# A two-layer streaming encoder whose VectorE runs in written order

## The chip, the cores and the metric

One core of a Trainium2 chip. The metric is the device time of one execution in microseconds (us), median of several runs. Engines: PE (TensorE, matmuls), DVE (VectorE), ACT (ScalarE), POOL (GpSimd), SP (SyncE, which issues the DMAs).

## The reference

One inference step of a hybrid encoder, float32, DEPTH = 2 layers, D_MODEL = 1024, on 512 frames of a new stream and 8 streams of 16 frames that go on from a cache: 640 columns in all. A layer, cut to what matters:

```python
h = rmsnorm(x, g_pre_mix)
u = h @ w_in                                   # conv, q, kv, z, x/B/C, dt and 3 gates
a = u_glu[..., :D_CONV] * jax.nn.sigmoid(u_glu[..., D_CONV:])
c = jax.nn.silu(layernorm(causal_dwconv(a_pad, conv_w, conv_b), conv_ln_g, conv_ln_b))   # 31 taps
o = attention(rmsnorm(u_q, g_q) @ w_uq, ...)   # latent attention, softmax over chunks
y = ssd(...)                                   # Mamba-2 scan in chunks of 64, then a gated rmsnorm
merged = gates[..., 0, :] * o_conv + gates[..., 1, :] * o_attn + gates[..., 2, :] * o_ssm
x = x + rmsnorm(merged @ w_out, g_post_mix)
f = rmsnorm(x, g_pre_ffn) @ w_gate_up
f = (jax.nn.silu(f[..., :D_FF]) * f[..., D_FF:]) @ w_down
x = x + rmsnorm(f, g_post_ffn)
```

## The kernel before, in words

**Data and matmuls.** Activations lie transposed, as 8 blocks of 128 channels x 640 columns, and are worked on in two halves of 256 (half 0) and 384 columns (half 1). Every matmul of a weight is made of three: weights and activations are split into a high and a low part (`split`, L141: ACT copies the high part, L142, and DVE or POOL subtracts it from the source, L136), and `mm3` (L122) sums high x high, high x low and low x high. Tiles named wh, hh, fh are high parts, wl, hl, fl low parts (wbh, wbl: weights in a second pool).

**Units.** A `Unit` (L215) is 128 output columns of a weight: `load` fetches it in pieces of 128x512 (`raw`) and splits them, on POOL or DVE as its argument `eng` says; `run(half)` puts 24 matmuls into one of four PSUM buffers (`pg`) and calls the unit's `evac`, which reads it. The feed-forward units of the first six column blocks (`gu`, L1308) alternate POOL and DVE for the split of their weights.

**Interleaving.** Beside the units the kernel writes small programs as generators in lanes: attention (`attn`), state-space scan (`ssd`) and its norm (`yn`), convolution taps (`convp`, `conv`, `sc`), and the norms at the edges of a sub-layer (`bar`, `bar2`). After each unit, `pump` (L269) lets each lane advance by its rate, so the order in which the kernel writes its instructions is a mixture set by these rates:

```python
        u.run(half, k == "B")
        ...
        pump(0.5 * u.nk / 8)
```

**Who orders what.** The framework under the kernel takes the written instructions, adds the semaphores and, before the change, reorders the instructions of every engine by a scheduler of its own. Each engine then takes its list in order.

**Names in the prediction.**
- `task_conv` (L898): 23 of the 31 taps of the depthwise convolution, each two `scalar_tensor_tensor` on DVE (through `stt`, L139): `cv<-pp`, 128x512, and its twin `cv<-sp`, 128x128, for the samples. Nobody reads the result until the branch's layernorm. `task_sconv` (L973) does the same for the scan's 4 taps (`sa`).
- `rsqrt` (L178): 12 tiny DVE operations in a chain (`rv`, `ri`, then `ry` and `ra` three times over), with a 13th at L191 where it has a factor. It reads a column sum `cs` of PE (`colsum`, L172), and PE spreads its result over the partitions as `rb` (`bcast`, L194).
- `task_attn` (L617): softmax with `p` (L646 to L648), which PE transposes (`tp`, L657). `q_unit` (L567) makes `qf`, the normed q. `ecs` is a decay of the scan.
- `barrier` (L322): the last projection before a norm runs as all half 0, then all half 1. `sq_acc` (L400) squares each result on ACT (`sq`) and sums the squares on DVE (`acc`). `postnorm` (L410) takes the column sum of acc, rsqrt and rb, then per block a product on DVE and an addition of the residual `xl` (`mo` after the mixer, `dn` after the feed-forward), then squares and a tree of sums (`psq`, L376). `prenorm` (L384) takes their column sum and rsqrt, then per block `ht` (DVE, L394) and its split into `hh` and `hl`. `bar_mix` (L1298) chains both for the mixer's end, and `bar_ffn` (L1341) for the end of the feed-forward part.
- `fg`: the evacuation of a gate or up unit (`gu`).

Of the kernel before, what the change touches and what calls it, by code (L numbers as in the profile page):

```python
# [1574 lines left out]
@with_exitstack  # L1575
def hybrid_encoder_kernel(ctx: ExitStack, tc: tile.TileContext, I, O):
    emit(tc, ctx, I, O)


def build(nc, arrays):  # L1580
    I = {k: nc.dram_tensor("in_" + k, v.shape, mybir.dt.from_np(v.dtype), kind="ExternalInput").ap() for k, v in arrays.items()}
    O = {k: nc.dram_tensor("out_" + k, s, F32, kind="ExternalOutput").ap() for k, s in _OUTS.items()}
    with tile.TileContext(nc) as tc:
        hybrid_encoder_kernel(tc, I, O)


def _unlayout(r):
# [26 lines left out]
```

## Time and profile before

| what | value |
|---|---|
| median of 3 runs | 2809.32 us (2806.63 to 2812.78) |
| profiled execution | 2803.95 us |
| its span in the trace | 2802.2 us |
| mean granted clock of PE | 0.984 |
| instructions | 47677 |
| DVE busy | 1541.8 us, 3334 instructions |
| ACT busy | 1095.5 us |
| POOL busy | 1031.5 us |

Times in the trace are from the span's start. Layer 0's mixer reaches to about 975 us, its feed-forward part to about 1475, layer 1's mixer to about 2370, its feed-forward part to the end. [...]

### The profile page before, as it was taken

How to read it: one execution, taken by the hardware profiler on the slowest of the kernel's cores; microseconds unless marked ns; L12 is line 12 of the kernel's file. 1: busy time of each engine (PE TensorE's matmuls, PEld its weight loads, DVE VectorE, ACT ScalarE, POOL GpSimd, SP SyncE). 2: the span in 40 equal slices, each digit the busy share in tenths (PEclk: the TensorE clock that was granted, in tenths of full speed). 3: DMA queues.
4: the chain of work that ended last, by engine and by line, in shares of the span. 5: the costliest groups of instructions: out<-in, count | busy, mean ns of one | idle time of the engine just before them, and what ended most of it. 6: DMA issues, size and time to landing. Idle time of an engine off the chain costs nothing. (4 is left out here: it accounts for less than half of the span.)

```text
span 2802.2 us, 47677 instructions
## 1 busy us (share of the span) xinstructions
PE 2677.2 (96%) x17652; PEld 2571.6 (92%) x17652; DVE 1541.8 (55%) x3334; ACT 1095.5 (39%) x2436; POOL 1031.5 (37%) x992
## 2 busy tenths in 40 slices
PE   6989989999999899999979999999999999999998
PEld 6988888989999899999979888888989998999998
DVE  6464678485575732333573747676565656323334
ACT  4434543543334532222444344544443244322222
POOL 5563545544435400000565444545534353000004
PEclk9999999999999999999989999999999999999999
DMA  5353232534554422222444532334436444322224
GB/s 155 113 175 111 84 113 92 171 101 143 177 185 136 157 83 75 73 78 75 124 151 129 164 102 89 117 115 135 139 101 227 133 129 154 91 76 71 79 71 131
DMA packets 248538, 337.82 MB, mean 121 GB/s; under 512 B 52465, under 2 KB 139057, under 8 KB 248305
## 3 DMA queue, kind: packets, MB, share of 16 engines
q1 hardware_dynamic: 246720, 333.75, 38.3%
q8 instruction: 139, 2.28, 0.3%
q10 hardware_dynamic: 1584, 1.02, 0.1%
q14 instruction: 95, 0.77, 0.1%
HBM read 268.73 MB, written 65.94 MB: 119 GB/s over the span
## 5 line engine op out<-in xcount | busy, mean ns | idle before, releaser
L136 POOL TENSOR_TENSOR wl<-raw,wh 128x512 fp32r<-128x512 f32 (+2 forms) x470 | 634.4, 1356 | 1487.1 <-ACT wh L142 1440.9
L120 PE MATMUL pg<-hh,wh 128*128 128x256 f32 (+1 forms) x3296 | 1051.7, 319 | 6.3 <-ACT hh L142 4.7
L120 PE MATMUL pg<-hh,wl 128*128 128x256 f32 (+1 forms) x3296 | 1029.2, 313 | 8.3 <-DVE wl L136 7.9
L120 PE MATMUL pg<-hl,wh 128*128 128x256 f32 (+1 forms) x3296 | 1031.0, 313 | 3.0 <-DVE hl L136 1.7
L142 ACT CAST wh<-raw 128x512 fp32r<-128x512 f32 (+1 forms) x696 | 422.6, 610 | 862.6 <-PE pg L120 763.8
L120 PEld LDWEIGHTS pg<-hh,wh 128*128 128x128 f32 x3296 | 632.8, 192 | 13.0 <-ACT hh L142 5.2
L120 PEld LDWEIGHTS pg<-hh,wl 128*128 128x128 f32 x3296 | 633.0, 192 | 9.6 <-DVE wl L136 8.7
L120 PEld LDWEIGHTS pg<-hl,wh 128*128 128x128 f32 x3296 | 633.0, 192 | 8.4 <-DVE hl L136 3.4
L136 DVE TENSOR_TENSOR wl<-raw,wh 128x512 fp32r<-128x512 f32 (+1 forms) x226 | 154.6, 684 | 293.7 <-ACT wh L142 293.5
L120 PE MATMUL pg<-fh,wh 128*128 128x256 f32 (+1 forms) x648 | 200.6, 310 | 0.0
L120 PE MATMUL pg<-fl,wh 128*128 128x256 f32 (+1 forms) x648 | 200.2, 309 | 0.0
L120 PE MATMUL pg<-fh,wl 128*128 128x256 f32 (+1 forms) x648 | 200.1, 309 | 0.0
L139 DVE SCALAR_TENSOR_TENSOR cv<-pp,pk,cv 128x512 f32<-128x512 f32 x184 | 152.4, 829 | 13.5 <-POOL cv L136 13.5
L120 PEld LDWEIGHTS pg<-fl,wh 128*128 128x128 f32 x648 | 122.0, 188 | 0.0
L120 PEld LDWEIGHTS pg<-fh,wl 128*128 128x128 f32 x648 | 121.9, 188 | 0.0
L120 PEld LDWEIGHTS pg<-fh,wh 128*128 128x128 f32 x648 | 121.9, 188 | 0.0
L136 POOL TENSOR_TENSOR cv<-cv,cvt 128x640 f32<-128x640 f32 x56 | 89.2, 1593 | 84.8 <-ACT cvt L893 74.7
L139 DVE SCALAR_TENSOR_TENSOR sa<-pd,pk,sa 128x664 f32<-128x664 f32 x96 | 100.9, 1052 | 15.3 <-ACT sa L982 14.3
L136 DVE TENSOR_TENSOR acc<-acc,sq 128x256 f32<-128x256 f32 (+1 forms) x96 | 65.1, 680 | 72.4 <-ACT sq L407 71.6
L136 DVE TENSOR_TENSOR fg<-fg,pg 128x256 f32<-128x256 f32 (+1 forms) x88 | 42.8, 486 | 98.3 <-PE pg L120 98.3
L139 DVE SCALAR_TENSOR_TENSOR cv<-sp,pk,cv 128x128 f32<-128x128 f32 x184 | 86.4, 469 | 0.0
L142 ACT CAST fh<-fg 128x256 fp32r<-128x256 f32 (+1 forms) x88 | 40.5, 460 | 107.4 <-DVE fg L136 104.2
(309 smaller groups left out, 4595.7 us busy)
## 6 DMA issues: line engine op xcount, KB each, us to landing
raw<-in_w_in SPq DMA_DIRECT2D x284, 256.0 KB, 2.9
raw<-in_w_gu SPq DMA_DIRECT2D x208, 256.0 KB, 2.7
raw<-in_w_down SPq DMA_DIRECT2D x72, 256.0 KB, 2.7
raw<-in_w_mix SPq DMA_DIRECT2D x64, 256.0 KB, 2.9
ma<-gd SPq DMA_DIRECT2D x48, 320.0 KB, 4.3
raw<-in_w_out SPq DMA_DIRECT2D x48, 256.0 KB, 2.8
gd<-gs SPq DMA_DIRECT2D x48, 192.0 KB, 2.4
hb<-in_state_ssm SPq DMA_DIRECT2D x64, 128.0 KB, 2.9
```

The source lines that it names most:

```text
L120: nc.tensor.matmul(ps, l, r, start=a, stop=b)
L136: eng.tensor_tensor(o, a, b, op=op)
L139: V.scalar_tensor_tensor(o, a, s, b, op0=op0, op1=op1)
L142: nc.scalar.copy(hi, src)
```

## The change

The kernel's body is written inside a context that tells the scheduler to leave DVE alone: DVE takes its instructions in the order in which the kernel writes them. The other engines are still ordered by the scheduler. No instruction of PE, DVE, ACT, POOL or of the DMAs is added or taken away.

```diff
--- before.py
+++ after.py
@@ -1581,7 +1581,8 @@
     I = {k: nc.dram_tensor("in_" + k, v.shape, mybir.dt.from_np(v.dtype), kind="ExternalInput").ap() for k, v in arrays.items()}
     O = {k: nc.dram_tensor("out_" + k, s, F32, kind="ExternalOutput").ap() for k, s in _OUTS.items()}
     with tile.TileContext(nc) as tc:
-        hybrid_encoder_kernel(tc, I, O)
+        with tc.manual_schedule(engines={mybir.EngineType.DVE}):
+            hybrid_encoder_kernel(tc, I, O)
 
 
 def _unlayout(r):
```

DVE's list has 3334 working instructions before and after, of which 1083 change their place relative to the rest (PE: 350 of 16520, by at most 41 places; ACT 289 of 2367; POOL 80; SP 144). Three places, with what was before first. In a row, the names are those of the section above, with the number of the tile and of its buffer's use.

**DVE in the middle of layer 0, two rsqrt chains (ry_1017 and ry_1021) that PE waits for.** Before:

```order
L136 TENSOR_TENSOR ra_1022_4776<-ra_1022_4776,rv_1019_4770 128x3
L139 SCALAR_TENSOR_TENSOR cv_879_4108<-pp_861_4023,pk_28_132,cv_879_4108 128x512
L136 TENSOR_TENSOR ra_1018_4759<-ra_1018_4759,rv_1015_4753 128x2
L139 SCALAR_TENSOR_TENSOR ry_1021_4774<-ra_1022_4776,ry_1021_4774 128x3
L139 SCALAR_TENSOR_TENSOR cv_879_4108<-sp_862_4024,pk_28_132,cv_879_4108 128x128
L139 SCALAR_TENSOR_TENSOR ry_1017_4757<-ra_1018_4759,ry_1017_4757 128x2
L139 SCALAR_TENSOR_TENSOR ra_1022_4776<-ry_1021_4774 128x3
L139 SCALAR_TENSOR_TENSOR cv_879_4108<-pp_861_4023,pk_28_132,cv_879_4108 128x512
L191 TENSOR_SCALAR ry_1017_4757<-ry_1017_4757 128x2
L136 TENSOR_TENSOR ra_1022_4776<-ra_1022_4776,rv_1019_4770 128x3
```

With the change:

```order
L136 TENSOR_TENSOR ra_1018_4761<-ra_1018_4761,rv_1015_4755 128x2
L139 SCALAR_TENSOR_TENSOR ry_1017_4759<-ra_1018_4761,ry_1017_4759 128x2
L139 SCALAR_TENSOR_TENSOR ra_1018_4761<-ry_1017_4759 128x2
L136 TENSOR_TENSOR ra_1018_4761<-ra_1018_4761,rv_1015_4755 128x2
L139 SCALAR_TENSOR_TENSOR ry_1017_4759<-ra_1018_4761,ry_1017_4759 128x2
L139 SCALAR_TENSOR_TENSOR ra_1018_4761<-ry_1017_4759 128x2
L136 TENSOR_TENSOR ra_1018_4761<-ra_1018_4761,rv_1015_4755 128x2
L139 SCALAR_TENSOR_TENSOR ry_1017_4759<-ra_1018_4761,ry_1017_4759 128x2
L191 TENSOR_SCALAR ry_1017_4759<-ry_1017_4759 128x2
L180 TENSOR_SCALAR rv_1019_4772<-cs_1014_4751 128x3
```

The taps (cv_879) that stood between the links are gone from here, and the second chain follows the first instead of being threaded into it.

**DVE at layer 0's mix barrier, the rsqrt of half 0's postnorm (rv_2141).** Before:

```order
L136 TENSOR_TENSOR acc_2064_9831<-acc_2064_9831,sq_2118_10082 128x256
L136 TENSOR_TENSOR acc_2064_9831<-acc_2064_9831,sq_2127_10124 128x256
L180 TENSOR_SCALAR rv_2141_10203<-cs_2130_10155 128x2
L182 TENSOR_SCALAR ri_2142_10205<-rv_2141_10203 128x2
L184 TENSOR_SCALAR ry_2143_10207<-ri_2142_10205 128x2
L139 SCALAR_TENSOR_TENSOR ra_2144_10209<-ry_2143_10207 128x2
L136 TENSOR_TENSOR ra_2144_10209<-ra_2144_10209,rv_2141_10203 128x2
```

With the change:

```order
L136 TENSOR_TENSOR acc_2064_9833<-acc_2064_9833,sq_2118_10084 128x256
L136 TENSOR_TENSOR acc_2064_9833<-acc_2064_9833,sq_2127_10126 128x256
L136 TENSOR_TENSOR acc_2129_10155<-acc_2129_10155,sq_2140_10202 128x384
L180 TENSOR_SCALAR rv_2141_10205<-cs_2130_10157 128x2
L182 TENSOR_SCALAR ri_2142_10207<-rv_2141_10205 128x2
L184 TENSOR_SCALAR ry_2143_10209<-ri_2142_10207 128x2
L139 SCALAR_TENSOR_TENSOR ra_2144_10211<-ry_2143_10209 128x2
```

The first partial sum of squares of half 1, acc_2129 (from sq_2140), has come ahead of the chain.

**DVE a little later in the same barrier, the low part wl_2265 of the first gate/up weights.** Before, in the middle of half 1's rsqrt chain (ry_2249):

```order
L136 TENSOR_TENSOR fg_2228_10599<-fg_2228_10599,pg_2244_10634 128x256
L139 SCALAR_TENSOR_TENSOR ry_2249_10668<-ra_2250_10670,ry_2249_10668 128x3
L136 TENSOR_TENSOR wl_2265_10740<-raw_2263_10737,wh_2264_10739 128x512
L136 TENSOR_TENSOR fl_2246_10660<-fg_2228_10599,fh_2245_10659 128x256
L139 SCALAR_TENSOR_TENSOR ra_2250_10670<-ry_2249_10668 128x3
```

With the change:

```order
L136 TENSOR_TENSOR psq_2258_10708<-psq_2258_10708,psq_2259_10709 128x384
L136 TENSOR_TENSOR psq_2252_10702<-psq_2252_10702,psq_2254_10704 128x384
L136 TENSOR_TENSOR psq_2256_10706<-psq_2256_10706,psq_2258_10708 128x384
L136 TENSOR_TENSOR psq_2252_10702<-psq_2252_10702,psq_2256_10706 128x384
L136 TENSOR_TENSOR wl_2265_10742<-raw_2263_10739,wh_2264_10741 128x512
L139 SCALAR_TENSOR_TENSOR fg_2268_10771<-ft_2267_10770,pg_2266_10745 128x256
L136 TENSOR_TENSOR wl_2274_10783<-raw_2272_10780,wh_2273_10782 128x512
```

It now stands behind the tree of sums psq_2252, the last of half 1's postnorm. **PE** with the change, around the column sum cs_2287 of that tree:

```order
L120 MATMUL pg_2284_10828<-hl_2167_10338,wh_2264_10741 128x256
L120 MATMUL pg_2294_10873<-hh_2158_10329,wh_2270_10776 128x256
L120 MATMUL pg_2294_10873<-hl_2159_10330,wh_2270_10776 128x256
L120 MATMUL cs_2287_10857<-c_ones_111,psq_2252_10702 128x1 x3
L120 MATMUL pg_2294_10873<-hh_2158_10329,wl_2271_10777 128x256
L120 MATMUL pg_2284_10828<-hh_2166_10337,wl_2265_10742 128x256
```

Before, cs_2287 stood 41 rows further down, in a later unit, behind all matmuls with wl_2265; now it stands ahead of them, in the middle of units pg_2284 and pg_2294.

## Rows read from the trace of the kernel before

**Rows 1.** The page, part 1: busy time, share of the span, instructions.

```profile
PE 2677.2 (96%) x17652; PEld 2571.6 (92%) x17652; DVE 1541.8 (55%) x3334; ACT 1095.5 (39%) x2436; POOL 1031.5 (37%) x992
```

**Rows 2.** Stretches by stage: length, busy us of PE, PEld, DVE, ACT, POOL, granted clock, DMA.

```profile
100.00:880.00 780.00, 750.31 (x4915) 702.78 (x4914) 495.21 (x1099) 333.25 (x783) 377.01 (x377) 0.99 0.42 131
880.00:975.00 95.00, 87.23 (x601) 85.36 (x601) 68.59 (x153) 47.81 (x105) 47.63 (x40) 0.98 0.50 160
975.00:1375.00 400.00, 400.00 (x2705) 400.00 (x2704) 140.28 (x248) 118.82 (x227) 31.18 (x27) 1.00 0.27 82
1375.00:1475.00 100.00, 84.13 (x541) 82.36 (x540) 71.19 (x163) 44.42 (x98) 60.64 (x51) 0.90 0.49 151
1475.00:2270.00 795.00, 768.50 (x5030) 719.04 (x5030) 484.99 (x1102) 340.20 (x797) 381.05 (x384) 0.99 0.42 132
2270.00:2370.00 100.00, 92.95 (x605) 91.11 (x604) 70.56 (x157) 47.38 (x102) 44.65 (x38) 0.95 0.49 156
```

**Rows 3.** PE's waits, 100 to 880 us: us in total, times, longest.

```profile
PE tp L657 <- DVE p L648: 8.1, 5, 4.2
...
PE rb L120 <- DVE ry L191: 3.6, 2, 2.3
...
PE pg L120 <- DVE qf L136: 2.7, 3, 2.0
PE rb L120 <- DVE ry L139: 1.8, 1, 1.8
```

**Rows 4.** The same, 1475 to 2270 us.

```profile
PE tp L657 <- DVE p L648: 4.4, 2, 3.6
PE rb L120 <- DVE ry L139: 4.3, 1, 4.3
PE opt L792 <- DVE ecs L139: 3.9, 1, 3.9
PE rb L120 <- DVE ry L191: 2.4, 2, 1.6
PE pg L120 <- DVE qf L136: 2.0, 2, 1.8
```

**Rows 5.** DVE's timeline in layer 0's middle: start, length, engine, line, operation.

```profile
439.22 0.15 DVE L139 SCALAR_TENSOR_TENSOR ra<-ry 128x3 f32<-128x3 f32 x1
439.29 0.74 DVE L139 SCALAR_TENSOR_TENSOR cv<-pp,pk,cv 128x512 f32<-128x512 f32 x1
...
440.03 0.15 DVE L136 TENSOR_TENSOR ra<-ra,rv 128x3 f32<-128x3 f32 x1
440.10 0.34 DVE L139 SCALAR_TENSOR_TENSOR cv<-sp,pk,cv 128x128 f32<-128x128 f32 x1
```

**Rows 6.** Three stretches of 10 us, columns as in rows 2.

```profile
440.00:450.00 10.00, 7.46 (x36) 7.16 (x37) 9.44 (x28) 0.85 (x2) 1.64 (x1) 0.83 0.31 116
940.00:950.00 10.00, 6.29 (x42) 6.08 (x40) 6.52 (x12) 5.15 (x12) 4.88 (x5) 0.83 0.66 217
1738.00:1748.00 10.00, 6.36 (x31) 6.29 (x31) 9.04 (x23) 4.47 (x10) 4.54 (x6) 0.66 0.52 145
```

**Rows 7.** DVE's timeline, layer 0's mix barrier, postnorm of half 0.

```profile
890.17 0.16 DVE L180 TENSOR_SCALAR rv<-cs 128x2 f32<-128x2 f32 x1 [2.33 <-PE cs L120]
...
893.11 1.14 DVE L136 TENSOR_TENSOR ra<-ra,rv 128x2 f32<-128x2 f32 x1
...
896.10 0.94 DVE L136 TENSOR_TENSOR acc<-acc,sq 128x384 f32<-128x384 f32 x1
```

**Rows 8.** The same, half 1, in order of time.

```profile
930.45 0.69 DVE L136 TENSOR_TENSOR wl<-raw,wh 128x512 fp32r<-128x512 f32 x1 [0.21 <-ACT wh L142]
...
947.26 0.55 DVE L136 TENSOR_TENSOR psq<-psq,psq 128x384 f32<-128x384 f32 x1
...
956.73 0.69 DVE L136 TENSOR_TENSOR wl<-raw,wh 128x512 fp32r<-128x512 f32 x1
...
964.97 0.60 DVE L139 SCALAR_TENSOR_TENSOR ht<-mo,pk,rb 128x384 f32<-128x384 f32 x1
```

**Rows 9.** PE's timeline in the same barrier: a matmul and the wait before it.

```profile
945.79 0.58 PE L120 MATMUL pg<-hh,wl 128*128 128x256 f32 x1 [3.71 <-DVE wl L136]
```

## The prediction

> **What bounds the kernel now.** I read the page's busy times first, then the stretches by stage, then who TensorE (PE) waited for in each stretch, then the timeline of VectorE (DVE) at those places. PE is busy for 2677.2 of 2802.2 us, DVE for 1541.8 [rows 1]. So PE is the bound, and DVE's order can only act through PE's idle time, 2802.2 − 2677.2 = 125 us, or through the clock that PE is granted. The stretches say where that idle time lies [rows 2]: none of it in 975 to 1375 us, the feed-forward matmuls, where PE is busy for 400.00 of 400.00 us; 7.8 us in 880 to 975 (the change from mixer to feed-forward, "mix barrier" below), 15.9 us in 1375 to 1475 (from feed-forward to the next layer) and 7.1 us in 2270 to 2370 (layer 1's mix barrier). About 30 us more lies in the middle of layer 0 and 27 us in that of layer 1, where attention, convolutions and the state-space branch run between the weight units.
>
> The profiled execution took 2803.95 us, 5.4 us under the median of the runs, 2809.32. The sum below is a difference made inside that one execution; I add it to the median.
>
> **What goes: taps ahead of short chains, in the middle of the layers.** In the middle stretches the waits of PE that a DVE instruction ended are mostly on the softmax result p (8.1 us in layer 0, 4.4 in layer 1), on the rsqrt chains (`ry`: 3.6 + 1.8, then 4.3 + 2.4), on qf (2.7, 2.0) and on ecs (3.9) [rows 3, 4], 33.2 us in all. The timeline shows why they were late [rows 5]: between two 0.15 us links of a rsqrt chain stands a convolution tap of 0.74 us with its 0.34 us twin for the samples, though no one waits for that tap for a long time. In the written order the chain stands unbroken and the taps come behind it (first piece of order above). I laid the recorded durations of DVE into the new order, every instruction starting when its operands of before were there and the one ahead was done, and read how much earlier the awaited instruction ends, up to the length of PE's gap. Softmax gives 0.6 + 1.3 + 3.2 + 0.8 = 5.9 us, the rsqrt chains 1.1 + 2.3 + 1.3 + 0.8 + 1.5 = 7.0, qf 0.4 + 2.0 + 1.8 = 4.2, ecs 1.4. Together 18.5, taken as **−19 us**. Bounds: 0, if the new order puts another late operand at the same place, and −33, all those waits.
>
> [...]
>
> **What comes: the mix barriers.** Here the scheduler had pulled short, urgent work ahead, and the written order puts it back behind work that is ready later. Per barrier, in layer 0's times:
> - Postnorm of the first column half. Its rsqrt starts at 890.17 and ends at 894.4, after one stretched operation of 1.14 us at 893.11 and one short one [rows 7]. Now `acc_2129`, a partial sum of the other half that starts at 896.10 (it needs a square of ScalarE that PE's next unit feeds), stands ahead of it, so the chain starts near 896.8 and rb comes about 6.5 us later. Behind the waiting acc on DVE stands nothing else that PE needs so soon. PE's list is made anew and carries 22 matmuls ahead of rb; at 601 matmuls in 87.23 us [rows 2] they cover 3.2 us: +3.3.
> - The sums of squares behind it (psq, then the column sum cs) are late by the same 6.5 us, less what PE has lost already and some idle time of DVE in front of them: +1.5, between 0 and 3.3.
> - Half 1. `wl_2265`, the low part of the first gate/up weights, ran on DVE at 930.45, between links of a chain. Now it stands behind the last sum `psq_2252`, which started at 947.26 [rows 8], and PE's list has the column sum cs_2287 in the middle of that weight unit. PE reaches that point some 4 to 5 us later than before (the two terms above), near 944, and psq and wl_2265 are done near 953, as they shift too: a gap of 9.3 us. The gap of 3.71 us of before at 945.79, for the next wl [rows 9], falls into it: +5.6.
> - `wl_2324` ran at 956.73, ahead of the eight prenorm pairs ht and hl; now it stands behind the last of them, which ran at 964.97 [rows 8]. 9.2 us late; PE's work for earlier units and the delay that it has by then cover about half: +4.
>
> That is 14.4 us, **+29 us** for two barriers; layer 1's list has the same pattern. [...] Bounds of the barriers: 0 if PE's new order covers all, and the full lateness 6.5 + 1.5 + 9.3 + 9.2 = 26.5 each if it covers none.
>
> [...]
>
> **The other edges.** The feed-forward barrier has the same code, but PE idles 15.9 us of it already [rows 2]; there the late chain partly takes the place of waits that are paid now. A third of a mix barrier: **+5** (0 to +14). At the start the parameters' transforms go ahead of the first sums of squares, and at the end the last postnorm is written serially: two to three stretched short operations each, of 1.14 us [rows 7]: **+4** together (−4 to +8). In the middle of the layers I count eight places where a unit's operand now stands behind one tap and its twin, 0.74 + 0.34 us [rows 5], or two of them: 8.6 to 17 us, near the low end since a part falls beside other waits: **+10** (0 to +17). In the two feed-forward stretches PE waits for no weight split, and DVE is busy for only 140.28 of 400 us [rows 2], so an order of its own finds it early enough: 0. If that cover went, each unit would wait for one split. No instruction is added or removed, and DMA issues on SP move only between their neighbours: 0.
>
> **Sum**: −19 − 8 + 29 + 6 + 5 + 4 + 10 = +27, or 2809.3 + 27 = **2836 us**, 1.0% slower.
>
> **The rivals.**
> - *Faster.* The place is the same mix barrier; the mechanism is PE's own list. It was ordered by a scheduler that knew DVE's fixed order, so the barrier's late operands may meet matmuls of other units where I count gaps. For it: 22 matmuls ahead of rb. Against: with cs_2287 and rb_2310 all of half 1 waits on one chain, and few units are left to place there. With barriers at 3 us each without more clock loss, 2 at the feed-forward barrier, 2 at the ends and 4 in the middle, the additions are 14 and the time is −27 + 14 = −13: 2796 us. It decides where all additions stay under 21 us.
> - *No change.* Gains and barrier losses cancel, additions of 21 to 33 us: 2809 us. That the change would do nothing belongs here, but the lists exclude it: about a third of DVE's 3334 instructions stand in another place relative to the rest.
> - *Much slower.* The waits are handed on whole at the barriers: 2 × 26.5 in place of 29, so +51: 2860 us. For it: DVE's queue is shared by weight splits and chains, and a late wl also holds a raw buffer and so a load. [...] Against: DVE is idle for 45% of the span, so that a late start is soon made up.
>
> **Chances.** The forecast 0.55, much slower 0.14, faster 0.18, no change 0.13. A measurement here can tell about 0.2% from no change, 5.6 us. So slower by more 0.69, within 0.13, faster 0.18. The forecast's own range is 2818 to 2855 (barrier terms 9 to 22 each, gains 19 to 33). For 8 in 10 the range goes down to the faster rival, 2796, and up to just past the slower, 2866; about one in ten is left out on each side.
>
> **What the profile would show.** Right: PE's waits on p, qf and ry in the two middle stretches shrink by some 19 us; PE idles 20 us or more in each mix barrier instead of 7 to 8, on rb, on a cs fed by psq and on pg fed by wl of DVE, with the granted clock lower there; the feed-forward stretches stay at 400 of 400. Wrong: mix barriers at 10 us or less (then faster), or the middle stretches no better (then slower than forecast), or gaps in the feed-forward stretches.

## The result, and the profile after

The changed kernel takes 2879.72 us (median of 4 runs, 2872.53 to 2882.63) against 2810.07 (2806.63 to 2812.78): a ratio of 1.0258 with a 95% interval of 1.0235 to 1.028, so some 70 us more. The forecast was 2836, with a range up to 2866: the direction was right and the size was less than half of it.

Where the time went is read from the page's busy times, the stretches by stage and PE's waits, in this order. The page of the changed kernel, profiled in an execution of 2882.63 us with a span of 2880.8:

```profile
PE 2695.3 (94%) x17652; PEld 2584.8 (90%) x17652; DVE 1588.8 (55%) x3334; ACT 1101.7 (38%) x2436; POOL 1008.5 (35%) x992
```

Of the 78.6 us by which the span grew, PE's idle time took 185.5 − 125.0 = 60.5 and PE's busy time 18.1, at the same 17652 matmuls [rows 1]. Most of the second part is, by my estimate, the clock. The granted clock stands at either 1.00 or 0.50 of the full one in both traces, and its mean is 0.972 where it was 0.984, which puts PE at 0.50 for some 161 us of the span in place of 90 (an estimate from the two means). Matmuls of 256 columns that follow each other every 0.12 us at 943 us, where the granted clock is 1.00, do so every 0.21 us at 963, where it is 0.50; over 71 us more, that is up to 30 us.

The stages of the changed kernel, with columns as in rows 2 (the stages start later, so the bounds differ):

```profile
...
900.00:1000.00 100.00, 76.47 (x502) 73.02 (x501) 67.51 (x150) 41.29 (x90) 37.27 (x32) 0.90 0.40 128
1000.00:1400.00 400.00, 400.00 (x2703) 400.00 (x2702) 136.66 (x248) 118.42 (x227) 30.73 (x26) 1.00 0.26 81
1400.00:1500.00 100.00, 74.21 (x463) 71.48 (x461) 66.19 (x146) 38.29 (x83) 53.48 (x48) 0.87 0.44 138
...
2320.00:2440.00 120.00, 96.70 (x601) 93.25 (x600) 68.80 (x153) 47.53 (x101) 45.56 (x39) 0.89 0.39 126
```

Layer 0's mix barrier now leaves PE 23.5 us idle in 100 us, and layer 1's 23.3 in 120, against 7.8 and 7.1 [rows 2]; between the layers it is 25.8 against 15.9; the feed-forward stretch is still busy for 400.00 of 400.00. How much each stage adds can be had more sharply, by the start of one and the same matmul in both timelines: at 100 us of the kernel before it comes 3.1 us earlier in the changed one, at 400 us 13.6 earlier, at 880 us 5.5 later, at 975 us 25.0 later, at 1375 us 25.4, at 1475 us 40.4, at 2270 us 51.5 and at 2370 us 72.7 later. The mix barriers cost 19.6 and 21.2 us, the passage between the layers 15.0, the feed-forward stretch 0.4. The middle of layer 0 first gained 10 us and then gave 19 back; layer 1's mixer lost 11.

Whom PE waited for, over the whole span (us in total, times, longest). The kernel before:

```profile
PE rb L120 <- DVE ry L139: 31.1, 15, 5.2
PE tp L657 <- DVE p L648: 12.5, 7, 4.2
...
PE cs L120 <- DVE psq L136: 7.5, 3, 4.7
...
PE sc L120 <- ACT p L646: 1.2, 2, 0.7
```

The changed kernel:

```profile
PE rb L120 <- DVE ry L139: 44.6, 18, 5.1
PE cs L120 <- DVE psq L136: 31.4, 6, 11.1
PE sc L120 <- ACT p L646: 17.3, 11, 6.5
PE pg L120 <- ACT sq L407: 10.4, 2, 5.3
PE tp L657 <- DVE p L648: 7.2, 7, 1.9
PE pg L120 <- ACT gt L853: 6.4, 1, 6.4
```

The wait on p at the transposes fell as forecast (12.5 to 7.2), but a wait that was next to nothing, of the score matmul on p (1.2), has become 17.3 us. The others that grew lie at the edges of the layers: rb on `ry`; cs on the sums `psq`, 11.1 us in each mix barrier; and two evacuations by ACT that were not waited for before, `sq` at the start and between the layers and `gt` between the layers.

PE's timeline in layer 0's mix barrier (start, us, operation, and in brackets the idle time before it and what ended it):

```profile
946.10 0.83 PE L120 MATMUL rb<-c_ident,ry 128*128 128x128 f32 x6
...
949.30 0.39 PE L120 MATMUL pg<-hh,wh 128*128 128x256 f32 x1 [0.96 <-ACT wh L142]
...
960.95 1.41 PE L120 MATMUL cs<-c_ones,psq 128*128 128x1 f32 x6 [11.14 <-DVE psq L136]
```

and DVE's at the same time:

```profile
939.71 0.42 DVE L139 SCALAR_TENSOR_TENSOR fg<-ft,pg 128x256 f32<-128x256 f32 x1 [0.52 <-ACT ft L1311]
...
941.86 1.23 DVE L136 TENSOR_TENSOR fl<-fg,fh 128x256 fp32r<-128x256 f32 x1 [0.47 <-ACT fh L142]
943.02 0.15 DVE L180 TENSOR_SCALAR rv<-cs 128x3 f32<-128x3 f32 x1
...
956.83 3.97 DVE L136 TENSOR_TENSOR psq<-psq,psq 128x384 f32<-128x384 f32 x4 [0.17 <-ACT psq L379]
...
961.32 0.41 DVE L139 SCALAR_TENSOR_TENSOR fg<-ft,pg 128x256 f32<-128x256 f32 x1
```

The column sum that half 1's chain reads was there at 939.9, but `rv` starts at 943.02, behind three evacuation steps of a gate/up unit (`fg`, `fg`, `fl`), two of which wait for ACT, and a weight split. The two chains of half 0 were held up as well, by partial sums of half 1 (`acc`) that stood ahead of them on DVE and waited for their squares:

```profile
901.18 0.98 DVE L136 TENSOR_TENSOR acc<-acc,sq 128x384 f32<-128x384 f32 x1 [8.90 <-ACT sq L407]
902.08 0.15 DVE L180 TENSOR_SCALAR rv<-cs 128x2 f32<-128x2 f32 x1
...
921.66 0.56 DVE L136 TENSOR_TENSOR acc<-acc,sq 128x384 f32<-128x384 f32 x1 [4.20 <-ACT sq L407]
922.14 0.15 DVE L180 TENSOR_SCALAR rv<-cs 128x2 f32<-128x2 f32 x1
```

The column sums for these two `rv` were there at 895.6 and 916.4, some 6 us earlier. From `rv` of half 1 to its last psq at 960.8 every step waits for the one before it: link by link, then the broadcast, then products, additions and sums. Meanwhile PE uses up its four PSUM buffers: two hold finished units that nobody has read yet, and two hold units that are begun and lack a low weight (`wl_2265` starts on DVE at 960.72, behind psq). cs is the next in PE's list at that point; the next evacuation, `fg` at 961.32, stands behind psq in DVE's list too. The gap of 11.14 us has no counterpart in rows 9, where 3.71 was the longest. The clock follows it, columns as in rows 2:

```profile
936.00:946.00 10.00, 9.05 (x70) 8.45 (x71) 7.66 (x21) 2.82 (x7) 4.11 (x3) 1.00 0.78 243
946.00:956.00 10.00, 2.85 (x23) 2.43 (x21) 7.03 (x13) 5.24 (x11) 5.95 (x6) 0.78 0.46 169
956.00:966.00 10.00, 5.05 (x26) 5.08 (x27) 8.00 (x12) 3.02 (x8) 3.35 (x4) 0.54 0.54 178
```

### The profile page after: what moved, and what is told of

Its sections match the earlier page's. It is cut to its first block, busy times and chain, and to the rows that moved or that the text cites. A ratio compares the mean times of both kernels' runs of the same rounds, so it can differ in the third digit from the quotient of the medians.

```text
span 2880.8 us, 47603 instructions
## 1 busy us (share of the span) xinstructions
PE 2695.3 (94%) x17652; PEld 2584.8 (90%) x17652; DVE 1588.8 (55%) x3334; ACT 1101.7 (38%) x2436; POOL 1008.5 (35%) x992
## 5 line engine op out<-in xcount | busy, mean ns | idle before, releaser
L136 POOL TENSOR_TENSOR wl<-raw,wh 128x512 fp32r<-128x512 f32 (+2 forms) x470 | 619.5, 1324 | 1534.2 <-ACT wh L142 1470.2
L136 DVE TENSOR_TENSOR wl<-raw,wh 128x512 fp32r<-128x512 f32 (+1 forms) x226 | 148.7, 687 | 88.9 <-ACT wh L142 88.5
L139 DVE SCALAR_TENSOR_TENSOR cv<-pp,pk,cv 128x512 f32<-128x512 f32 x184 | 167.5, 910 | 0.0
L139 DVE SCALAR_TENSOR_TENSOR fg<-ft,pg 128x256 f32<-128x256 f32 (+1 forms) x88 | 42.8, 487 | 192.3 <-ACT ft L1311 192.3
L139 DVE SCALAR_TENSOR_TENSOR cv<-sp,pk,cv 128x128 f32<-128x128 f32 x184 | 105.5, 573 | 0.0
```

Source lines behind the costliest of these rows:

```text
L136: eng.tensor_tensor(o, a, b, op=op)
L139: V.scalar_tensor_tensor(o, a, s, b, op0=op0, op1=op1)
```

## The experiments

Ratios are to the kernel before, run on the same chip, with their 95% interval; us are the ratio's excess times 2810.

**Middle alone, edges alone.** A helper turns DVE's written order on and off at chosen units. The first kernel has it on only from the last unit of the entering norm to the projection w_out, in both layers; the second has it on everywhere else.

```diff
+    held = []
+    def order(on):
+        if on and not held:
+            held.append(tc.manual_schedule(engines={mybir.EngineType.DVE}))
+            held[0].__enter__()
+        elif not on and held:
+            held.pop().__exit__(None, None, None)
...
-            add_hook(lambda: (flush("bar"), flush("bar2")))
+            add_hook(lambda: (flush("bar"), flush("bar2"), order(True)))
...
+            add_hook(lambda: order(False))
             barrier([wout(m) for m in range(8)], KEEP_W[1], bar_mix, us[-KEEP_W[2]])
```

> Written order of VectorE holds only in the middle of each layer (from the first attention weight units to the last unit of the branches' projections); around the three barriers, the start and the end the scheduler orders VectorE again. Theory A, the places add up: by the profile of the change the two middles cost 8.5 and 11.0 us over the kernel before, so about 2810 + 20 = 2830 us, and the mix barriers are back at 7 to 8 us of PE idle. Theory B, the places are coupled (the losses of the middles come from the backlog that the barriers leave): the middles show the gains alone, 2810 us or less. Theory of the prediction (middles -19 of waits, -8 of clock, +10 new waits): 2793 us.

> The complement: written order of VectorE at the start, around the barriers and through the feed-forward parts, the scheduler's order in the middle of the layers. Theory A: the barriers, the start and the end cost what they cost under the change, 19.6 + 21.3 + 15 - 3 + 6 = 59 us, so about 2869 us. Theory B: the barriers are cheaper when the middles hand them a kernel that is in the scheduler's order, under 2845 us. Theory of the prediction: +44, 2854 us.

Middle alone: 0.9991 [0.9979, 1.0003], which can't be told from no change. Edges alone: 1.0271 [1.0255, 1.0286], +76 us. The two add up to the whole change, but not as theory A had it, which took the cost of each place from the lag of its stage. By the lag the two middle stages cost 8.6 and 11.1 us in the changed kernel; in the trace of the edges alone, where these stages go by the scheduler, they cost 11.5 and 13.4, half of it or more in their first 125 us. So most of that lag belongs to the edges, whose region reaches into these stages. Two of PE's waits in the first kernel (its lines stand 8 further down):

```profile
PE sc L120 <- ACT p L654: 17.3, 11, 6.5
...
PE tp L665 <- DVE p L656: 7.3, 7, 2.0
```

They are those of the changed kernel, so the middle contains the gain and the new wait together, and they cancel. What makes the new wait is seen in the changed kernel's timeline, layer 0, before the 6.5 us; the first line is PE's score matmul that DVE's maximum reads:

```profile
402.75 0.59 PE L120 MATMUL sc<-k,al 128*128 128x256 f32 x2
...
408.11 0.74 DVE L139 SCALAR_TENSOR_TENSOR cv<-pp,pk,cv 128x512 f32<-128x512 f32 x1
408.77 1.61 DVE L139 SCALAR_TENSOR_TENSOR cv<-sp,pk,cv 128x128 f32<-128x128 f32 x1
410.31 0.74 DVE L139 SCALAR_TENSOR_TENSOR cv<-pp,pk,cv 128x512 f32<-128x512 f32 x1
410.97 0.34 DVE L139 SCALAR_TENSOR_TENSOR cv<-sp,pk,cv 128x128 f32<-128x128 f32 x1
...
411.46 0.42 DVE L613 TENSOR_REDUCE mx<-sc 128x1 f32<-128x256 f32 x1
```

From the score matmul to the maximum, some 8 us, DVE works through a tap and its twin, four steps of the scan, and two more taps and twins; ACT's exponential, and behind it PE's next score matmul, wait for it. Two of the three twins take 1.66 and 1.61 us, at 404.18 and 408.77, where 0.34 is usual; POOL has an addition of `cv` under way at both, 2.04 us from 403.65 and 1.78 from 408.45, and none at the third (the last section has more such steps). The written order keeps taps out of one chain and puts them ahead of the next step of softmax.

**Which part of the edges.** The region only from w_out to the first six pairs of gate and up units (both mix barriers), and only from layer 0's last down projection to layer 1's first k unit.

```diff
+            add_hook(lambda: order(True))
             barrier([wout(m) for m in range(8)], KEEP_W[1], bar_mix, us[-KEEP_W[2]])
             add_halves(us, KEEP_W[2])
+            add_hook(lambda: order(False))
```

> Written order of VectorE only from the last projection of the mixer to the end of the first six pairs of gate/up units, in both layers; the scheduler's order elsewhere. Theory L, the edges add up: the lag under the change grows by 19.6 and 21.3 us there, so 2809 + 41 = 2850 us. Rival M, the loss comes from delays that each edge hands to the next: 2830 us or less.

> Written order only from the last down projections of layer 0 to the first attention weight units of layer 1. Theory L: the lag under the change grows by 15 us there, and by some 3 more at the key, query and latent norms that follow: 2809 + 18 = 2827 us. Rival M: 2815 us or less. With e13, theory L leaves 70 - 41 - 18 = 11 us to the start and the last barrier.

Mix barriers: 1.0163 [1.0132, 1.0193], +46 us (37 to 54). Between the layers: 1.0067 [1.0048, 1.0085], +19 us (13 to 24). Together 65 of the 76; the rest, the kernel's start and end, was not run alone. In the traces the end costs some 6 us: behind 2745 us of the kernel before, the lag grows by 6.2 us more in the changed kernel and by 5.7 with the edges alone. In the first, matmuls of the two barriers come 21.3 and 20.2 us later, as in the changed kernel, with the same gap:

```profile
PE cs L120 <- DVE psq L136: 30.8, 7, 11.1
```

**The low weights on POOL.** My prediction put 5.6 us of each barrier on the column sum and wl_2265 of DVE, behind the sums. Here POOL makes all low weights of these units.

```diff
-    E_OUT, E_GU, E_DN = (G, G), (G, V), (G, G)
+    E_OUT, E_GU, E_DN = (G, G), (G, G), (G, G)
```

> The changed kernel, with the splits of the first six pairs of gate/up weights all on GpSimd rather than on GpSimd and VectorE in turn. Theory A: the wait for the low weight parts that stand behind the postnorm's sums and behind ht/hl goes, so of the 11.1 us gap at the column sum of each mix barrier some 5 remain, and the 2.8 us at the later weight goes: about 2880 - 2 x 9 = 2862 us. Rival: GpSimd, which also has a share of the barrier's additions and splits, becomes the one that is late, and the gaps stay with another releaser: 2875 us or more.

1.0255 [1.0239, 1.027], as the changed kernel. The gap stays without any wl on DVE there:

```profile
964.85 1.41 PE L120 MATMUL cs<-c_ones,psq 128*128 128x1 f32 x6 [11.35 <-DVE psq L136]
```

So wl_2265 is not the only thing that holds PE. Between rb and cs PE now does some 40 matmuls of units in place of 14, until all four buffers hold finished units at 953.5, whose evacuations stand behind psq. What wl_2265 alone is worth the run doesn't show: POOL now makes splits between the chain's additions, and the last psq ends at 964.7 in place of 960.8.

**A fifth PSUM buffer for the units,** one fewer for the other tiles; also on the kernel before, as a control.

```diff
-    psg = pool("psg", 4, space=bass.MemoryType.PSUM)
-    psb_ = pool("psb", 4, space=bass.MemoryType.PSUM)
+    psg = pool("psg", 5, space=bass.MemoryType.PSUM)
+    psb_ = pool("psb", 3, space=bass.MemoryType.PSUM)
```

> The changed kernel with five PSUM buffers for the units and three rather than four for all the rest. Theory G: one further unit of 24 matmuls, 3 us, fits into each of the waits with full buffers: the column sum's gap falls from 11.1 to 8 us in each mix barrier, the two waits on ScalarE's evacuations between the layers (5.3 and 6.4 us) by 3 each, and the middles pay a little for the buffer they lose: 2880 - 10 = 2870 us. Rival H: the gaps stay, since what PE waits for is not a buffer: 2880 us or more.

> The kernel before with the same five and three PSUM buffers, the control for the run above. Theory G: its gaps of 3.7 us in the mix barriers, where a weight split of VectorE comes late, are not buffer waits and stay, so the time is that of the kernel before, give or take what the lost buffer costs the middles, 2805 to 2820 us.

With the change 1.0246 [1.0229, 1.0263], without it 0.9994 [0.9983, 1.0005]. The gap shrank by 2.8 us, and a wait ahead of it grew from 0.96 to 2.04:

```profile
950.29 0.58 PE L120 MATMUL pg<-hh,wh 128*128 128x256 f32 x1 [2.04 <-ACT wh L142]
...
959.40 1.41 PE L120 MATMUL cs<-c_ones,psq 128*128 128x1 f32 x6 [8.32 <-DVE psq L136]
```

But from rb to cs PE takes as long as in the changed kernel (944.56 to 959.40; there 946.10 to 960.95), with 16 matmuls of units in between in place of 14. The fifth buffer takes a fifth unit, whose first low weight is as late as those of the other two that are begun. The ratio is 3 us below that of the changed kernel, which is within the noise.

**Letting units in between the barrier's steps.** A pause between the additions and the sums, in place of one behind the sums, so that evacuations come between them.

```diff
-BY = 2
+BY = 1
...
+            yield
```

> The changed kernel with a pause in the postnorm between the residual additions (mo, dn) and the sums of squares (psq), and one pause fewer behind them, so that in written order one gate/up evacuation and one weight split stand between the two parts. Theory G: PE stops at the barriers because its four PSUM buffers are full, and the evacuation that would free one stands behind the whole chain on VectorE; now it stands some 6 us earlier, so the 11.1 us gap at the column sum falls to 5 to 8 us: 2880 - 2 x 4 = 2872 us, or less if the barrier between the layers gains too. Rival H: the evacuation in the chain's middle delays the chain by what it waits for, and the gap moves to the next column sum: 2880 us or more.

1.0274 [1.026, 1.0288], no gain. The wait on psq fell from 11.14 to 3.03, and one on a weight split, here of POOL, took its place:

```profile
954.23 1.13 PE L120 MATMUL pg<-hh,wl 128*128 128x256 f32 x2 [6.81 <-POOL wl L136]
...
962.07 1.41 PE L120 MATMUL cs<-c_ones,psq 128*128 128x1 f32 x6 [3.03 <-DVE psq L136]
```

The three runs go together: a late chain holds back the evacuations and the low weights at once, and where one of the two was taken away, the other held PE.

**The prenorm's alternation.** In the written order each block's `ht` is followed by its own `hl`, which needs ACT's high part. The changed kernel, then the kernel before, half 0 of the mix barrier:

```profile
926.68 0.47 DVE L139 SCALAR_TENSOR_TENSOR ht<-mo,pk,rb 128x256 f32<-128x256 f32 x1
927.62 0.42 DVE L136 TENSOR_TENSOR hl<-ht,hh 128x256 fp32r<-128x256 f32 x1 [0.47 <-ACT hh L142]
...
936.17 0.42 DVE L136 TENSOR_TENSOR hl<-ht,hh 128x256 fp32r<-128x256 f32 x1 [0.47 <-ACT hh L142]
```

```profile
919.47 0.87 DVE L139 SCALAR_TENSOR_TENSOR ht<-mo,pk,rb 128x256 f32<-128x256 f32 x2
920.25 1.27 DVE L136 TENSOR_TENSOR hl<-ht,hh 128x256 fp32r<-128x256 f32 x1
...
925.09 0.41 DVE L136 TENSOR_TENSOR hl<-ht,hh 128x256 fp32r<-128x256 f32 x1
```

The scheduler had put one to three `ht` ahead of each `hl`, and half 0 took 7.6 us (917.88 to 925.50); written, it takes 10.3, with DVE idle at each handover. So the code was changed to run `ht` two blocks ahead, in the changed kernel, and then four.

```diff
+AHEAD = 2
...
-                split(hh[:, c], hl[:, c], tmp, G if k % 4 == 3 else V)
...
+            for k in range(8 + AHEAD):
...
+                if k >= AHEAD:
+                    n = k - AHEAD
+                    hh, hl = L["h"][n]
+                    split(hh[:, c], hl[:, c], tmps[n], G if n % 4 == 3 else V)
```

> The changed kernel, but the prenorm is written so that VectorE makes two further blocks of ht before it splits the first. Theory A: the ping-pong between VectorE and ScalarE (0.47 us of idle per block of half 0, 0.58 of half 1) goes; half 0 of the barrier between the layers takes 9 us rather than 12, and PE waits less for ht/hh/hl: 5 prenorms x 2 to 3 us, 2868 us. Rival: PE waits at the barriers for the rsqrt chains ahead of it, and the prenorm's own pace is hidden: within 3 us of 2880.

> The changed kernel with the prenorm four blocks ahead instead of two. Theory N: most of the loss is in the chains, and more distance takes out more of it: 2855 us or less. Theory O: two blocks already hide ScalarE's 0.47 us, so four give nothing more: 2864 us, give or take 4.

Two ahead: 1.0206 [1.0182, 1.023], about 15 us of the loss gone (5 to 24); four: 1.0222 [1.0192, 1.0252], nothing more. The gap of 11.1 stayed, so this is a second cause beside it.

**Twice the pace of the norms' lanes,** without and with `ht` two ahead.

```diff
-    rate = dict(bar=2.0, bar2=2.0, attn=RATE[0], ...
+    rate = dict(bar=4.0, bar2=4.0, attn=RATE[0], ...
```

> The changed kernel with the two lanes of the norms (bar, bar2) advanced twice as fast, so that VectorE's written order has the rsqrt of half 0's postnorm ahead of the other half's sum of squares, and that of half 1 ahead of the second gate/up evacuation and its split. Theory C, formed from the first four runs: the mix barrier is lost because the chain of half 1 (rsqrt, mo, psq) starts late behind half 0's prenorm and behind evacuations, while PE's four PSUM buffers fill up, whose evacuations in turn stand behind that chain on VectorE; started a unit earlier, the 11.1 us gap at the column sum shrinks by 4 to 6 us in each mix barrier and the feed-forward barrier gains as much: about 2880 - 16 = 2864 us. Rival D: the gap comes from where the scheduler places the column sum in PE's list, and stays at 11 us: 2875 us or more.

> Faster norm lanes and the prenorm written two blocks ahead, together, in written order throughout. Theory C: the two effects add up, since one starts the chain earlier and the other shortens the piece ahead of it: 2864 - 16 = 2848 us. Rival D: only the shorter prenorm counts, 2864 us.

1.0334 [1.0312, 1.0357] and 1.028 [1.0264, 1.0295]: the theory that the chain only has to be written earlier fell. The gap at cs was 9.8 us, but PE's waits on the squares became 11.4 us in one piece and those on POOL's wl 10.0; `ht` ahead was worth as much as before, 15 us.

```profile
PE pg L120 <- ACT sq L407: 11.4, 1, 11.4
```

**The norms' chains alone in written order.** Each step of the two barrier lanes is its own region; what stands between (units, their evacuations, weight splits, taps) goes by the scheduler.

```diff
+        if lane in ("bar", "bar2"):
+            order(True)
+        try:
+            return step1(lane)
+        finally:
+            order(False)
```

> Written order only inside each piece of the norms at the edges (rsqrt, additions, sums of squares, prenorm), every piece a region of its own; evacuations, sums of squares of the projections, weight splits and all other work are placed around and between by the scheduler. Theory N: the loss is the order inside the chains, above all ht and hl in turn: 2809 + 55 or more. Theory O: it is that the chains and the work of other units stand in one fixed row, so that whichever waits holds up the other; with that freed, only the prenorm's alternation is left, and part of it is filled with other work: 2809 + 5 to 16 us, 2825 us at most.

> Written order only inside the pieces of the norms, as in the run before, with the prenorm written two blocks ahead. Theory P: the alternation of ht and hl is all that written order costs inside the chains; 2825 - 16 = 2809 us, within 0.3% of the kernel before. Rival Q: the chains cost something else too (rsqrt, additions and sums written in one go where the scheduler threads other work in): 2818 us or more.

1.0076 [1.0047, 1.0105] and, with `ht` two ahead, 1.0041 [1.0027, 1.0055]. Some 50 of the 70 us are thus not in the order inside a norm step, but in where the steps stand among the units' evacuations and splits. What remains shows PE waiting on evacuations:

```profile
PE pg L120 <- DVE fg L139: 15.2, 4, 7.3
```

The alternation is not all of these last 21 us: with `ht` ahead 12 (8 to 15) remain. How much it is stays open, since the two intervals overlap.

**The pace of the taps in the middle.** In the kernel with the middle alone, the convolution lane at 2.0 and 6.0 steps in place of 3.0.

```diff
-RATE = (1.4, 1.3, 1.2, 3.0, 3.0, 1.0)
+RATE = (1.4, 1.3, 1.2, 2.0, 3.0, 1.0)
```

> Written order in the middles only, with the convolution taps written at two thirds of the rate (one tap and its twin after each unit rather than one or two). Theory E: in written order the middles give back what they gain because pairs of taps stand ahead of the score tile's mask, maximum and exponential (waits of PE's score matmuls on ScalarE's p, 17 us under the change, 1 before); with fewer taps ahead those waits fall by half and the time to about 2797 us. Rival F: VectorE is short of time there rather than badly ordered; the taps only move to the end of the middle, and the time is that of the run with the old rate, 2804 us, or more.

> The same with twice the old rate: bursts of three taps and their twins, done earlier. Theory E: every burst is some 3 us ahead of a softmax or scan step that PE waits for, so its waits grow by 10 us or more: 2814 us or more. Rival F: the order within the middle does not matter as long as the work is done: 2804 us.

1.0152 [1.0137, 1.0167] and 1.0085 [1.0068, 1.0102]: both slower, both expectations missed in part. At 2.0 the taps end late, and the branch's layernorm is waited for:

```profile
PE cs L120 <- DVE acc L136: 25.3, 7, 5.7
PE mb L120 <- DVE lns L136: 22.2, 3, 9.9
```

At 6.0 the score's wait fell from 17.3 to 7.7, and others came, 8.4 on a load and 6.9 on DVE's `zt`:

```profile
PE sc L120 <- DMA al<-qd: 8.4, 2, 4.4
...
PE sc L120 <- ACT p L654: 7.7, 7, 3.1
```

**Only the k, v and q units in written order,** where the changed kernel had gained.

```diff
-            add_hook(lambda: lanes["attn"].append(task_attn()))
+            add_hook(lambda: (order(False), lanes["attn"].append(task_attn())))
```

> Written order only for the first units of each middle (keys, values and queries), the scheduler's order everywhere else. Theory I, from the run with written order in both middles: there the lag behind the kernel before goes from -1.2 to -7.5 us in layer 0 and from -0.7 to -6.8 in layer 1 in just this piece, and what follows gives it back; kept alone, the piece gives 2 x 6 = 12 us: 2796 us where the kernel before has 2808. Rival J: the gain is only time borrowed from later waits on VectorE's load, and is given back under the scheduler's order too: 2805 us or more.

0.9983 [0.9972, 0.9994], the lowest ratio of all, but the theory fell: PE was 5.06 us ahead of the kernel before where this piece begins and 5.05 where it ends, so the piece itself gave nothing. The lead was there from 75 us on, ahead of the piece, and what gained is not known.

## Why the prediction was right or wrong

- **Direction, and where:** right. PE idles over 20 us in each mix barrier, on rb, cs and pg, at a lower clock, and not at all in the feed-forward stretches.
- **The mix barriers, +29 and +6 of clock:** the mechanism was right, and the sizes nearly. Forecast 35, measured 19.6 + 21.2 in the changed kernel and 46 (37 to 54) alone. In layer 0, rb of half 0's postnorm cost PE 1.95 us (forecast 3.3), the column sum ahead of wl_2265 11.14 less the 3.71 of before, so 7.4 (forecast 5.6), and two later low weights 2.47 and 2.75 (forecast 4 for wl_2324). What the term for cs left out is that the four PSUM buffers can't be emptied either while psq is ahead on DVE; with the low weights on POOL that held PE, and the time stayed. The prenorm's handovers, ht to ACT to hl, I had not priced at all; they are worth some 15 us over all edges.
- **"The feed-forward barrier ... a third of a mix barrier: +5":** failed. I took PE's idle time there as room that the late chain would fill. It cost 15 us in the trace and 19 alone, almost as much as a mix barrier, because the waits came in addition: on the squares (`sq`, 5.3) and on a gate's activation (`gt`, 6.4). ACT makes both, but its list holds them behind squares and `hh` casts that wait for the chain on DVE and POOL: the cast ahead of `gt`, at 1500.54, waits 1.15 us for its `ht`.
- **"eight places ... +10", against −19 and −8:** this is the step with the largest error. The −19 came: in the two middle stages of the kernel with the middle alone, the waits that it counted (p, `ry`, qf, ecs) fell from 33.2 to 14.7 us. The term of +10 for new waits failed: all waits that grew there add up to 39 us, 16 of them on the score matmul. I had looked for operands of weight units behind a tap, and not for links that reach PE through ACT. The middle came out at −3 (−6 to +1) and not at −17.
- **Clock:** forecast −8 + 6. Both were my estimates, and no run shows either term; what the traces show is PE's busy time, which grew by 18.1 us in place of falling by 2, a mean granted clock of 0.972 in place of 0.984, and 956 to 966 us at 0.54.
- **Start and end, +4:** not run alone; the end cost some 6 us in two traces, and the start can't be told from nothing.
- **"Much slower", +51:** of the rivals it was nearest, but only in the number. On DVE the trace shows a late step passed on: `rv` at 902.08 starts only behind the `acc` that had waited 8.90 us, though its column sum was there at 895.6. That such a wait is handed on whole to PE it doesn't show: this chain was some 6 us late and PE waited 1.95 us for its rb, and the two barriers cost 41 us in the trace, not the rival's 53 with 6 of clock. That the total came near the rival's was luck: what it lacked lay in the middle and between the layers, which it left as in the forecast. I had counted on PE's new list to cover a part: it covered half 1's rb (no wait at 946.10), and 3 us later the buffers and the low weights were used up.

The errors in summary: −17 for the middle became −3 (14 us), +5 between the layers became 15 to 19 (10 to 14), the mix barriers were 6 to 11 larger, and the end some 2. That is 32 to 41 of the 43 us; the rest is not placed.

No run held the lists of the other engines as they were, which the scheduler made anew, so the loss is that of the change as a whole and not of DVE's list alone.

## What to carry to other kernels

An order in which a short chain stands unbroken still has to put the long work somewhere: look at what then stands ahead of the next awaited link, and follow that link through the other engines to PE, ACT above all. Where one engine, in one fixed row, empties the matmuls' PSUM buffers, splits their weights and runs the chain that the next norm needs, a late chain holds back all three, as at the gap of 11.14 us: one more buffer (1.0246, where the change alone has 1.0258), or the splits on another engine (1.0255), gave nothing here by itself. Taking away one such wait (a buffer, a split, a pause, another pace) moved it to the next operand each time; letting a producer run two blocks ahead of a step that goes through a second engine was the one edit that paid in the written order (1.0206).

## What the runs showed that was not expected

Links of a rsqrt chain, mostly 0.16 us each, took 1.17 to 1.20 us five times in a row between the layers. The changed kernel's DVE and POOL timelines there:

```profile
1476.84 1.17 DVE L184 TENSOR_SCALAR ry<-ri 128x3 int32<-128x3 int32 x1
...
1481.73 1.19 DVE L139 SCALAR_TENSOR_TENSOR ra<-ry 128x3 f32<-128x3 f32 x1
1482.95 0.16 DVE L136 TENSOR_TENSOR ra<-ra,rv 128x3 f32<-128x3 f32 x1
```

```profile
1476.70 6.20 POOL L136 TENSOR_TENSOR wl<-raw,wh 128x512 fp32r<-128x512 f32 x5 [3.79 <-issue]
```

Five splits of POOL in a row, 1.24 us each, and five links as long as one of them; the sixth, behind the last, is short again. The chain just ahead of it, from 1474.19 us on, ran while POOL stood idle, and has no long link. By the five long links this chain of 12 took some 5 us more. The change did not bring them in: the kernel before has two links of 1.14 us in the chain of rows 7, at 890.56 and 893.11, and four of 0.79 to 1.19 us in a chain at 1457 us. POOL has splits under way there as well: 1.28 us from 890.39, 1.29 from 892.94, and 1.18 and 3.70 us, one behind the other, from 1456.87. Long links and splits stand together in time, but no run took POOL's work away: that the splits make the links long was not shown.
